# Taking the 2 KB strip off the first load of a DMA-bound rotation

## The chip, the core and the metric

The kernel runs on one core of a Trainium2 chip. The metric is the time of one execution on the device in microseconds (us). Repeated executions lie within some 0.3% of each other. The "span" of a profile runs from the first to the last instruction of the core; the measured times are some 1.8 us longer.

## The reference

```python
x = np.random.randn(32, 3, 256, 256).astype(np.float32)
def reference(x):
    return np.rot90(x, k=2, axes=(-2, -1)).astype(np.float32)
```

A rotation by 180 degrees reverses the 65,536 values of each of the 96 images. 25.17 MB go in and 25.17 MB come out. Nothing is computed.

## The kernel before

The 96 images are handled in three groups of 32. A group lies in the SBUF, the core's own memory, as 128 partitions of 16,384 floats (64 KB): each image takes four partitions. VectorE, one of the core's compute engines, reverses each partition in place, block by block, through a small tile T. The store then writes the four partitions of an image in reverse order.

```python
E = L // 4            # 16384 floats, one partition of a group
J = E // 8            # 2048, a block of the copies
N = E // 32           # 512 floats: the 2 KB strip
...
def load(t, g, lo=0, hi=E):
    nc.sync.dma_start(out=t[:, lo:hi], in_=x4[g][:, lo:hi])
def store(t, g):
    nc.sync.dma_start(out=o4[g][:, ::-1, :], in_=t[:, :])
def inside(t):
    for lo in range(0, E // 2, J):
        hi = E - lo - J
        copy(T[:, :], back(t, hi, hi + J))
        copy(t[:, hi:hi + J], back(t, lo, lo + J))
        copy(t[:, lo:lo + J], T[:, :])

load(A, 0, 0, N)      # the strip: 128 rows of 2 KB
load(A, 0, N, E)      # the rest of group 0: 128 rows of 62 KB
load(Bt, 1)
load(Ct, 2)
for g, t in enumerate((A, Bt, Ct)):
    inside(t)
    store(t, g)
```

There is a tile for each group, so no load waits for a tile to come free. Loads and stores are all issued by the sync engine, on one queue.

## Time and profile before

| | before |
|---|---|
| time, median of the first 3 runs | 123.02 us (122.84 to 123.25) |
| span of the profile | 121.1 us |
| VectorE busy | 44.2 us, 36% |
| the DMA queue's packets, share of 16 engines' span | 97.4% |
| DMA transfers | 7: two for load A, one each for loads B and C, three stores |

The profile is read here in three ways. The page gives shares and the landing time of each transfer, counted from its issue. The windows give what the DMA engines moved in a stretch. The packet records of the trace give each row's start and duration: the large rows, sorted by start and taken sixteen at a time, one for each DMA engine, show the kernel as 48 rounds. The page's lines stand in the prediction below.

### The profile page before, as it was taken

Reading aid. Unit: us, or ns where it says so; the run is one execution under the profiler, and the core shown is the slowest. Engines: PE = TensorE matmul, PEld = TensorE weight load, DVE = VectorE, ACT = ScalarE, POOL = GpSimd, SP = SyncE. Lnnn points to the kernel's source line nnn. Section 1 sums busy time; section 2 is a strip of 40 time slices with the busy share of each in tenths; the row PEclk is TensorE's granted clock in tenths of the full one; section 3 lists DMA queues with packets and bytes.
Section 4 is the critical chain, followed back from the end, with each engine's and each line's share of the span. In section 5 each row is a group of like instructions: output and inputs, shape, how many; then the busy total and the mean of one; then the engine's idle time right before and its main releaser. Section 6 shows DMA issues by size and latency. Waiting matters only on the chain.

```text
span 121.1 us, 94 instructions
## 1 busy us (share of the span) xinstructions
DVE 44.2 (36%) x36; POOL 0.2 (0%) x4
## 2 busy tenths in 40 slices
DVE  0000000599994199998039999600000000000000
POOL 0000000000000000000000000000000000000000
DMA  9977987897799879978989977997799779977980
GB/s 359 399 336 336 650 356 336 346 693 346 346 411 628 346 346 476 563 346 346 346 346 476 563 346 346 563 476 346 346 584 455 346 346 606 433 346 346 671 368 0
DMA packets 1008, 50.33 MB, mean 416 GB/s; under 512 B 112, under 2 KB 112, under 8 KB 240
## 3 DMA queue, kind: packets, MB, share of 16 engines
q1 hardware_dynamic: 1008, 50.33, 97.4%
HBM read 25.17 MB, written 25.17 MB: 416 GB/s over the span
## 4 chain that ended last, share of the span: by engine, by line
DMA 33%; DVE 25%; another core or an unknown queue 4%; issue 1%; SPq 1%; DVEq 0%
DMA Bt<-in_x_dram 33%; DVE T L53 8%; DVE Ct L53 8%; DVE Bt L53 8%; SPq L56 1%; DVEq L53 0%
## 5 line engine op out<-in xcount | busy, mean ns | idle before, releaser
L53 DVE COPY T<-A 128x2048 f32<-128x2048 f32 x4 | 4.9, 1227 | 22.7 <-DMA A<-in_x_dram 22.6
L53 DVE COPY T<-Ct 128x2048 f32<-128x2048 f32 x4 | 4.9, 1227 | 5.4 <-DMA Ct<-in_x_dram 5.3
L53 DVE COPY T<-Bt 128x2048 f32<-128x2048 f32 x4 | 4.9, 1227 | 4.4 <-DMA Bt<-in_x_dram 4.3
L53 DVE COPY Bt<-T 128x2048 f32<-128x2048 f32 x4 | 4.9, 1227 | 0.1
L53 DVE COPY A<-T 128x2048 f32<-128x2048 f32 x4 | 4.9, 1227 | 0.1
L53 DVE COPY Ct<-Ct 128x2048 f32<-128x2048 f32 x4 | 4.9, 1227 | 0.1
L53 DVE COPY Bt<-Bt 128x2048 f32<-128x2048 f32 x4 | 4.9, 1227 | 0.1
L53 DVE COPY A<-A 128x2048 f32<-128x2048 f32 x4 | 4.9, 1227 | 0.1
L53 DVE COPY Ct<-T 128x2048 f32<-128x2048 f32 x4 | 4.9, 1227 | 0.1
L89 POOL MEMSET const-bfloat16-1.0<- 128x1 bf16 x1 | 0.1, 101 | 0.0
L89 POOL MEMSET const-uint8-127<- 128x1 uint8 x1 | 0.1, 101 | 0.0
L89 POOL MEMSET const-float32-0.0<- 128x1 f32 x1 | 0.1, 98 | 0.2 <-issue 0.2
L89 POOL MEMSET const-float32-1.0<- 128x1 f32 x1 | 0.1, 98 | 0.0
## 6 DMA issues: line engine op xcount, KB each, us to landing
A<-in_x_dram SPq DMA_DIRECT2D x1, 7936.0 KB, 21.4
A<-in_x_dram SPq DMA_DIRECT2D x1, 256.0 KB, 2.8
Bt<-in_x_dram SPq DMA_DIRECT2D x1, 40.3
Ct<-in_x_dram SPq DMA_DIRECT2D x1, 60.3
out_dram<-A SPq DMA_DIRECT2D x1, 43.9
out_dram<-Bt SPq DMA_DIRECT2D x1, 43.8
out_dram<-Ct SPq DMA_DIRECT2D x1, 42.7
```

The costliest lines, as they stand in the source:

```text
L53: tc.keep_in_program_order(nc.vector.tensor_copy(out=dst, in_=src))
L56: nc.sync.dma_start(out=t[:, lo:hi], in_=x4[g][:, lo:hi])
L89: nc = _bacc.Bacc("TRN2", target_bir_lowering=False, num_devices=1)
```

## The change

The intent is one transfer and one issue fewer: load A becomes one transfer of 8 MB like the others.

```diff
-    N = E // 32
...
-    def load(t, g, lo=0, hi=E):
-        nc.sync.dma_start(out=t[:, lo:hi], in_=x4[g][:, lo:hi])
+    def load(t, g):
+        nc.sync.dma_start(out=t[:, :], in_=x4[g])
...
-    load(A, 0, 0, N)
-    load(A, 0, N, E)
+    load(A, 0)
     load(Bt, 1)
     load(Ct, 2)
```

## The prediction

> **What bounds the kernel now.** I read the first parts of the page for the shares, then the issues with their landing times, then the windows, to see whether the DMA engines ever run below their full rate.
>
> ```profile
> span 121.1 us, 94 instructions
> DVE 44.2 (36%) x36; POOL 0.2 (0%) x4
> ...
> DMA packets 1008, 50.33 MB, mean 416 GB/s; under 512 B 112, under 2 KB 112, under 8 KB 240
> ...
> q1 hardware_dynamic: 1008, 50.33, 97.4%
> ...
> A<-in_x_dram SPq DMA_DIRECT2D x1, 7936.0 KB, 21.4
> A<-in_x_dram SPq DMA_DIRECT2D x1, 256.0 KB, 2.8
> Bt<-in_x_dram SPq DMA_DIRECT2D x1, 40.3
> Ct<-in_x_dram SPq DMA_DIRECT2D x1, 60.3
> out_dram<-A SPq DMA_DIRECT2D x1, 43.9
> ```
>
> VectorE (DVE) works for 36% of the span, the one DMA queue for 97.4%. Of the 1,008 packets, 112 are under 512 B (16 for each of 7 transfers: the completion marks), 128 are the strip's 2 KB rows, and 768 are whole rows of 62 or 64 KB. The landing times run from each issue. Load C is issued at 2.11 us in the timeline and lands at 62.4. The store of A is issued at 37.76 us and lands at 81.7, although its data were ready at 37.7: it stood behind load C. So the queue is served in order, and a store gets its turn long after it was issued.
>
> The windows show the same. Columns: stretch, its length, VectorE busy (instructions), GpSimd busy, clock, DMA share, GB/s.
>
> ```profile
> 1.70:2.60 0.90, 0.00 (x0) 0.00 (x0) 1.00 0.72 162
> ...
> 6.00:22.00 16.00, 0.00 (x0) 0.00 (x0) 1.00 1.00 430
> ...
> 41.00:58.00 17.00, 14.72 (x12) 0.00 (x0) 1.00 1.00 432
> 58.00:62.00 4.00, 0.00 (x0) 0.00 (x0) 1.00 1.46 508
> ...
> 81.00:119.00 38.00, 0.00 (x0) 0.00 (x0) 1.00 1.00 433
> ```
>
> Loads alone (6 to 22, 41 to 58) and stores alone (81 to 119) run at 430 to 433 GB/s with a DMA share of 1.00. There is no idle stretch to fill. (A window counts a packet's bytes where it ends, so the 508 is an edge effect.) The page's chain of waits puts 33% on load B and 25% on VectorE copies, but this is the chain of issues; the store that it leads to was issued at 77.59 us while the queue still had some 42 us of work. I do not take it as the bound. **The bound is the bytes through the queue, from the first packet to the last.**
>
> In the trace's packet records, each of the 16 DMA engines moves 8 strip rows, then 48 large rows one after the other, the next within a few ns of the end of the one before. A 64 KB row takes 2.418 us, a 62 KB row 2.342 us, a strip row 0.084 us. Sum for one engine: 8 x 0.084 + 8 x 2.342 + 40 x 2.418 = 116.1 us. First packet at 1.75 us, last end at 119.97: 118.2 us in all. The 2.1 us beyond the sum are start-up (0.6 us), one slow last row of load C on every engine (mean 3.55 instead of 2.418 us, so 1.1 us, where loads turn to stores), and the engines' spread of some 0.5 us, of which the mean engine sees half.
>
> **What the Trainium skill says.** (1) "DMA: Bandwidth & Descriptors", section "Where 436 GB/s comes from": 16 ports of 256 bits at 850 MHz give 435.2 GB/s. The trace agrees: 16 x 65,536 B in 2.418 us is 433.7 GB/s. Full rows are already at that ceiling, so the change cannot make a row faster. (2) The same page, "Queues, rings and completion order": on each engine descriptors are consumed in ring order. The landing times above agree. (3) The same page, "Anatomy of one DMA", gives a fixed cost of about 2 us for each DMA, measured there on the other issuing path and mostly completion latency. Were that paid in series, one DMA fewer would save about 2 us. This trace disagrees: the small transfer is followed on each engine by the next row within some 10 ns of its completion mark. (4) "SBUF — State Buffer", "SBUF: two separate sides": DMA and compute engines do not contend. The trace agrees: 432 GB/s with VectorE busy 14.72 of 17 us, 433 with it idle.
>
> **The change, part by part.**
> - *One issue fewer on the sync engine.* The two issues of A take 0.86 us together in the timeline, so about 0.43 us leaves the sync engine before load B is issued. Load B's rows are not wanted before about 21 us. Worth 0.
> - *The strip's 128 rows and 16 marks go.* Per engine 8 x 0.084 + 0.009 = 0.68 us, on the path.
> - *The 8 rows of load A grow from 62 to 64 KB.* Per engine 8 x (2.418 - 2.342) = 0.61 us, on the path. The bytes are the same; net of these two, -0.07 us.
> - *The start-up is met by 64 KB rows instead of 2 KB rows.* Before: the first strip row starts at a mean of 1.92 us over the engines, the first large row at 2.954. That is 1.03 us for rows that take 0.67 at the steady pace, so 0.36 us lost (18 of the 128 rows took over 0.1 us, some 0.6). The first round of 62 KB rows took 2.562 on average, another 0.22 lost. Together 0.58 us. After: the same start at 1.92, since the first issue does not move, and then one loss L on the first round of 64 KB rows. I cannot read L from this trace. Nothing lost would be L = 0; if the two losses were simply merged, 0.58; the worst stall this trace has is 1.1 us. I choose 0.45: large rows should hide part of the first latency that the short rows showed in full.
> - *The sum.* Before, the first row of load B starts at a mean of 21.967 us. After: 1.92 + 8 x 2.418 + 0.45 = 21.71, so 0.25 us earlier; with L from 0 to 1.1 between 0.7 earlier and 0.4 later. Everything after it (40 rows per engine at 2.418, the turn from load to store, the tail of 1.1 us after the last packet) stands as it is and moves along. 123.02 - 0.25 is 122.8 us.
> - *VectorE* starts its first copy when A is in, now at 22.63 us, then at about 22.4; the first store is issued at about 37.5 instead of 37.8. Its turn in the queue comes at about 61.5. Worth 0.
>
> **The rivals.**
> 1. *The strip is a primer that earns its place.* Whoever tuned this kernel put it there. Without it, all 16 engines begin with a 64 KB read at once, perhaps in closer step, and stall more. For it: the first round after the strip ran unevenly (2.342 to 2.949 us), and the spread of the engines' starts (0.47 us in the first large round, 0.36 between first strip packets) is set up by the strip. Against it: load B and load C are whole-row transfers with the same addresses' spacing, and run at the full 2.418 us. A stall also spreads the engines by itself. If true as a one-time cost: 0.5 to 1 us, so 123.3 to 124. If every load row of A slowed by 10%: 8 x 0.24 = 1.9 us, 124.9; to lose 2% (2.46 us) would need more than that, or a slowdown that lasts into B and C.
> 2. *Each transfer has a fixed price in series.* Then about 2 us are saved, 121 us. The gapless packets speak against it. Even with L = 0 and no strip, only 0.7 us is available, under 0.6%; so faster by 2% is all but ruled out.
> 3. *A later start is hidden or absorbed.* If the first 0.2 us gained were met by a queue running dry before the first store, they would be lost again. But the store of A is issued 24 us before its turn, the store of C at 77.6 us while A's store is still moving. So a gain or a loss at the front goes straight through to the end, and the result should be the front's difference, plus noise.
> 4. *The slow round where loads turn to stores changes.* It costs 1.1 us on every engine and I do not know what causes it. If it depended on how the engines stand to each other, it could shrink or grow by some tenths. This widens the range both ways.
>
> **Range and chances.** The three runs of before lie within 122.84 to 123.25, so the noise is about 0.2 us. L from 0 to 1.1 gives -0.7 to +0.4 us, the turn and noise add some 0.3 either way, and rival 1 adds weight above. Predicted 122.8 us, 8 times in 10 between 122.3 and 123.6. Faster by over 2% (below 120.6) 0.01, within 2% 0.94, slower by over 2% (above 125.5) 0.05, which is rival 1 in its lasting form.
>
> **What would show it.** In the profile after: 864 packets (1,008 less 128 strip rows and 16 marks), none between 512 B and 8 KB, the same 50.33 MB; one issue of A that lands some 21.5 us later, and the first copy at 22.2 to 22.6 us. Windows of loads alone and stores alone still at 430 to 433 GB/s. The first rows of load A at 2.418 plus about 0.45 us, all later ones but the last of load C at 2.418. The prediction is wrong if rows of load A take clearly more than 2.418 us beyond the first round, if loads B or C change pace, if the slow round at the turn changes by more than some tenths, or if the end does not move by what the first copy moved.

## The result, and the profile after

| | before | after |
|---|---|---|
| median of 6 runs each | 122.83 us (122.78 to 123.25) | 122.91 us (122.80 to 123.01) |
| span of the profile | 121.1 us | 121.2 us |
| load B's first row, mean start over the 16 engines | 21.967 us | 21.946 us |
| slow last row of load C, mean | 3.550 us | 3.549 us |
| end of each engine's last row, mean | 119.72 us | 119.69 us |

The ratio of the times is 0.9999 (95% interval 0.9984 to 1.0014). It is the same.

The page after, with the lines that answer to those of before in the prediction:

```profile
span 121.2 us, 91 instructions
DVE 44.2 (36%) x36; POOL 0.2 (0%) x4
...
DMA packets 864, 50.33 MB, mean 415 GB/s; under 512 B 96, under 2 KB 96, under 8 KB 96
...
q1 hardware_dynamic: 864, 50.33, 97.4%
...
A<-in_x_dram SPq DMA_DIRECT2D x1, 21.8
Bt<-in_x_dram SPq DMA_DIRECT2D x1, 40.7
Ct<-in_x_dram SPq DMA_DIRECT2D x1, 60.7
out_dram<-A SPq DMA_DIRECT2D x1, 44.1
```

The 128 strip rows and their 16 marks are gone from the packets, and the bytes are unchanged. The landing times of loads B and C seem to be 0.4 us later, but they are counted from issues that now come 0.45 us sooner (load B at 1.18 instead of 1.63 us). On the clock of the span they land where they did. The timeline shows the issues:

```profile
0.73 0.39 SPq L55 DMA_DIRECT2D A<-in_x_dram  x1
1.18 0.42 SPq L55 DMA_DIRECT2D Bt<-in_x_dram  x1
1.64 0.43 SPq L55 DMA_DIRECT2D Ct<-in_x_dram  x1
22.57 1.23 DVE L52 COPY T<-A 128x2048 f32<-128x2048 f32 x1 [22.57 <-DMA A<-in_x_dram]
```

The first copy starts at 22.57 us; before it was 22.63. So nearly nothing was gained at the front. The windows of the kernel after (stretch, its length, VectorE busy, GpSimd busy, clock, DMA share, GB/s):

```profile
1.70:2.60 0.90, 0.00 (x0) 0.00 (x0) 1.00 3.49 1165
...
6.00:22.00 16.00, 0.00 (x0) 0.00 (x0) 1.00 1.00 434
...
41.00:58.00 17.00, 14.72 (x12) 0.00 (x0) 1.00 1.02 439
58.00:62.00 4.00, 0.00 (x0) 0.00 (x0) 1.00 1.34 475
...
81.00:119.00 38.00, 0.00 (x0) 0.00 (x0) 1.00 0.99 428
```

The long stretches still move at the full rate. A row's bytes are counted whole where it starts, not where it ends as the prediction said. That is why the first window has 1165 GB/s (sixteen rows of 64 KB begin in it), and why the others stray by a few per cent from 433: one round more or less at an edge. For anything finer the packet records decide.

They say where the start-up went. Before, the first large rows began at 2.954 us and took 2.563 us on average instead of 2.342; in front of them the strip's rows had taken 0.95 us for each engine instead of 0.67. After, the first large rows began at 1.899 us and took 3.140 us on average instead of 2.418. From the next round on, each row took 2.418 us until the turn to the stores. So the first round lost 0.72 us where the strip (0.28) and the round after it (0.22) had lost 0.50.

### The profile page after: what moved, and what is told of

Read it like the earlier page. It is cut to its first block, busy times and chain, and to the rows that moved or that the text cites. A ratio compares the mean times of both kernels' runs of the same rounds, so it can differ in the third digit from the quotient of the medians.

```text
span 121.2 us, 91 instructions
## 1 busy us (share of the span) xinstructions
DVE 44.2 (36%) x36; POOL 0.2 (0%) x4
## 4 chain that ended last, share of the span: by engine, by line
DMA 34%; DVE 25%; another core or an unknown queue 4%; issue 1%; SPq 0%; DVEq 0%
DMA Bt<-in_x_dram 34%; DVE T L52 8%; DVE Bt L52 8%; DVE Ct L52 8%; SPq L55 0%; DVEq L52 0%
## 6 DMA issues: line engine op xcount, KB each, us to landing
out_dram<-A SPq DMA_DIRECT2D x1, 44.1
```

## The experiments

The theory: the strip's own price in the steady stream is about 0.07 us, and its place at the head saves about as much of the start-up, so that taking it away moves nothing; what the front gains or loses goes through to the end. The rivals: each transfer has a large fixed price in series, which the start-up hid; the strip is a primer worth more than its cost; slack further back absorbs the gain. The first four kernels ran on one chip with eleven runs of the kernel before (median 122.90 us), the next four with eleven (122.96), the last four with eleven or twelve (122.99). All twelve gave right results.

The columns below come from the packet records: the mean start of load B's first row (where the front ends), the mean duration of the last load row in front of each turn from loads to stores, and the mean end of the engines' last rows.

| run | load B begins, us | last large load row before a turn, us | last rows end, us | time, us | ratio to before (95%) |
|---|---|---|---|---|---|
| before | 21.967 | 3.55 | 119.72 | 122.83 | |
| after | 21.946 | 3.55 | 119.69 | 122.91 | 0.9999 |
| tail | 21.950 | 3.76 | 119.89 | 123.14 | 1.0012 (1.0000 to 1.0024) |
| narrow | 22.351 | 3.56 | 120.12 | 123.56 | 1.0046 (1.0031 to 1.0061) |
| wide | 21.910 | 3.65 | 119.97 | 123.04 | 1.0010 (0.9998 to 1.0022) |
| sixteen | 23.123 | 2.42 | 119.80 | 123.44 | 1.0048 (1.0033 to 1.0062) |
| delay | 26.378 | 3.59 | 124.18 | 127.47 | 1.0362 (1.0343 to 1.0381) |
| cturn | 21.911 | 3.30 (62 KB) | 119.67 | 123.05 | 1.0012 (0.9992 to 1.0033) |
| actst | 21.936 | loads and stores mixed | | 132.45 | 1.0763 (1.0733 to 1.0794) |
| moredve | 21.921 | 3.60 | 119.72 | 123.43 | 1.0029 (1.0009 to 1.0049) |
| latec | 21.996 | 3.42 | 119.62 | 122.94 | 0.9999 (0.9982 to 1.0015) |
| latebc | 21.924 | 3.63 | 119.75 | 123.03 | 1.0005 (0.9990 to 1.0021) |
| order | 21.976 | 2.97 and 2.49 | 119.20 | 122.69 | 0.9982 (0.9963 to 1.0002) |
| order_strip | 21.950 | 3.19 and 2.46 | 119.37 | 122.74 | 0.9977 (0.9960 to 0.9993) |

Seven kernels load A in one undelayed transfer (after, cturn, moredve, actst, latec, latebc, order). Their load B begins at 21.911 to 21.996 us, 21.944 on average. The two profiles with the 2 KB strip at the head have 21.967 and 21.950. The difference of 0.01 us is smaller than the spread among equal fronts.

**The strip at the other end of load A (tail).**

```diff
-    load(A, 0, 0, N)
-    load(A, 0, N, E)
+    load(A, 0, 0, E - N)
+    load(A, 0, E - N, E)
```

> The strip at the tail of load A instead of at its head: the first rows are large ones as in the changed kernel, and the strip's own price is met in the steady stream. Theory (the strip costs what its rows take, 0.68 us per engine, less 0.61 us that the large rows shrink by, and its place at the head bought back some 0.1 us of start-up): the first round loses about 0.72 us as in the changed kernel, load B's first row starts at a mean of about 22.0 us, time within 0.2 us of both kernels. Rival (each transfer has a fixed price of about 2 us in series, which the strip at the head hid in the start-up): about 125 us, with a gap or slow rows at about 21 us. Rival primer (the strip at the head saves as much as it costs): 0.1 us slower than the changed kernel, not to be told from the theory by the time, only by the packet records.

The issues of this run (size, us from issue to landing):

```profile
A<-in_x_dram SPq DMA_DIRECT2D x1, 7936.0 KB, 21.2
A<-in_x_dram SPq DMA_DIRECT2D x1, 256.0 KB, 21.4
```

The strip was issued right behind the large part and landed behind it. All of its 128 rows took less than 0.1 us, 0.084 in the median. Load B began at 21.950 us. A fixed price of 2 us in series is ruled out. The time was 0.12% (0.15 us) over before. In this profile the slow row at the turn was 0.2 us longer than in before, which would account for it; whether the strip had a part in that is not known.

**Other strip widths at the head (narrow, wide).**

```diff
-    N = E // 32
+    N = E // 128      # narrow: 512 B rows
+    N = E // 4        # wide: 16 KB rows
```

> Strip rows of 512 B instead of 2 KB, at the head. Theory: the rows take about 0.03 us each, 8 per engine 0.22 us, and the large rows shrink by 0.15; the start-up loss is between 0.5 and 0.75 us as with either kernel; time within 0.3 us of before. Rival primer by amount of data (the strip hides start-up in proportion to its bytes): the start-up loss is near the 0.72 us of no strip. Rival primer by number of rows: near 0.58 us.

> Strip rows of 16 KB instead of 2 KB, at the head. Theory: the steady price of a split is the same 0.07 us; the start-up loss between 0.58 and 0.72 us; time within 0.3 us of before. Rival primer by amount of data: start-up loss below 0.58 us, time up to 0.4 us less than before.

The narrow strip missed its expectation of 0.3 us: 0.46% is 0.57 us. First its windows, then those of the kernel before:

```profile
1.70:2.20 0.50, 0.00 (x0) 0.00 (x0) 1.00 0.44 130
2.20:2.60 0.40, 0.00 (x0) 0.00 (x0) 1.00 5.36 1789
2.60:3.60 1.00, 0.00 (x0) 0.00 (x0) 1.00 0.86 325
```

```profile
1.70:2.20 0.50, 0.00 (x0) 0.00 (x0) 1.00 0.67 78
2.20:2.60 0.40, 0.00 (x0) 0.00 (x0) 1.00 0.79 266
2.60:3.60 1.00, 0.00 (x0) 0.00 (x0) 1.00 2.87 1133
```

With 512 B rows the engines are busy for 0.44 of the first window, then wait: the last sixteen strip rows ended between 2.10 and 2.25 us, and the first large rows began at 2.23 at the earliest and 2.565 on average. The issue of the large part starts at 1.16 us, 0.43 after that of the strip; the first rows of each issue follow it by 1.0 to 1.1 us (1.753 after 0.73, 2.232 after 1.16). A strip that is done sooner than the next issue takes effect leaves the engines dry, here for some 0.4 us. The last sixteen rows of the 2 KB strip ended between 2.92 and 3.18 us, so it is long enough not to. The narrow strip did not soften the start-up either: its first round of large rows took 3.007 instead of 2.399 us. These 0.4 us are still there where load B begins (22.351 instead of 21.967) and in the mean end of the last rows; the rest of the 0.57 is not accounted for. The wide strip had the same front as no strip to within 0.04 us, so more bytes in the strip save nothing. Neither is a better primer.

**Load A in sixteen transfers (sixteen).**

```diff
-    load(A, 0, 0, N)
-    load(A, 0, N, E)
+    for k in range(16):
+        load(A, 0, k * (E // 16), (k + 1) * (E // 16))
```

> Load A as 16 transfers of 4 KB rows. Theory (a split costs only its additional packets, some 8.4 ns each, worked out from 84 ns for 2 KB against 2.342 us for 62 KB, and 9 ns for each completion mark): 120 more rows and 15 more marks per engine, 1.0 + 0.14 us, so about 1.1 us slower than before, 123.9 us. The 16 issues of some 0.43 us run ahead of rows that take 1.28 us per transfer. Rival (a fixed price of 2 us for each transfer in series): about 30 us slower, 153 us.

The front lost what was expected: load B began at 23.123 us, 1.18 later than in the kernel after, for 15 more transfers and 120 more rows per engine. So a split is cheap, some 0.08 us for a transfer with 8 rows per engine. But the time was only 0.48% over before. The slow last row of load C, 3.55 us in the two kernels compared, took 2.42 here. This gave back 1.1 us and was not foreseen. In the profiled execution (123.24 us, the fastest of its four and 0.35 over the profiled one of before) the last rows ended at a mean of 119.80 us, 0.08 later than in before; 0.30 of the 0.35 is the stretch from the last packet to the end of the span, 1.43 instead of 1.13 us.

**A front that is late by a known amount (delay).**

```diff
+    tc.keep_in_program_order(nc.vector.memset(A[:, :E // 4], 0.0))
     load(A, 0)          # the kernel after; its loads kept in program order
```

> The changed kernel with a 128x4096 memset on VectorE that load A waits for, so that the whole stream starts later by the memset's time (some 2 to 4 us, worked out from 1.23 us for a 128x2048 copy). Theory (the stream is gapless from its first row to its last, so what the front gains or loses reaches the end undiminished): start-up loss again about 0.72 us, the end moves by as much as the first row moved, within 0.2 us. Rival (slack further back absorbs what the front loses): the end moves by clearly less.

Its timeline:

```profile
1.65 3.47 DVE L67 MEMSET A<- 128x4096 f32 x1 [1.65 <-PEq L88]
5.15 0.38 SPq L55 DMA_DIRECT2D A<-in_x_dram  x1
```

The first row moved from 1.740 to 6.160 us, by 4.42. Load B moved by 4.43, the mean end of the last rows by 4.48. The ratio of 1.0362 on 122.96 us is 4.45 us. The stream has no slack: what the front loses is lost at the end. That a gain would pass in the same way is argued from the same gapless rows and not tested, but no gain had to be absorbed: load B began only 0.02 us sooner.

**More work on VectorE (moredve).**

```diff
             copy(T[:, :], back(t, hi, hi + J))
+            copy(T[:, :], back(t, hi, hi + J))
```

> The changed kernel with each first copy done twice: 4.9 us more VectorE work per tile, so stores are issued at about 42.6, 62 and 82.5 us. Theory (VectorE has over 20 us of slack): within 0.2 us of before. As to the slow last row of load C: if it goes with the issue of store B, which then falls 4.9 us later, after the turn, the slow row moves or goes, worth up to 1.1 us; if it goes with the turn itself, it stays at about 3.55 us.

4.9 us more for each tile, 14.7 us in all, moved the time by 0.29%, some 0.4 us, with an interval of 0.1 to 0.6. That is more than the 0.2 us expected, but the excess does not lie where VectorE works: the spans of the four executions are 121.0 to 121.3 us, as those of before in the same rounds (121.0 to 121.6), and the mean end of the last rows was 119.72 us, as in before. The time outside the span was 2.2 us instead of 1.8 in all four; why is not known. Inside the span VectorE has its slack. The slow row stayed at 3.60 us, so it does not go with the issue of store B.

**The turn from loads to stores (cturn, latec, latebc, order, order_strip).** The run with sixteen transfers had shown that the slow row is not a fixed price. It is equal before and after, so it is no part of the change's result; but it is 1.1 us, more than anything the strip could be worth.

```diff
# cturn: the kernel after, the strip cut from the tail of load C
-    load(Ct, 2)
+    load(Ct, 2, 0, E - N)
+    load(Ct, 2, E - N, E)
# latec: load C issued only when A is in
# (here and in latebc the loads are kept in program order)
+    copy(Ct[:, :1], A[:, :1])
     load(Ct, 2)
# latebc: loads B and C issued late
+    tc.keep_in_program_order(nc.vector.memset(Bt[:, :], 0.0))
     load(Bt, 1)
+    tc.keep_in_program_order(nc.vector.memset(Ct[:, :E // 16], 0.0))
     load(Ct, 2)
# order: load C queued behind store A (order_strip: the same, with the strip)
-    load(Ct, 2)
         store(t, g)
+        if g == 0:
+            load(Ct, 2)
```

> The changed kernel with the 2 KB strip cut from the tail of load C, so that strip rows and not a large row are the last before the stores. Theory A (the slow last row of 3.55 us is a fixed wait for the first store rows): the strip rows carry about 1.1 us of wait, time within 0.2 us of the changed kernel plus 0.07. Theory B (the large row is slowed in proportion while stores begin behind it): the wait falls to some 0.04 us and the time to about 121.9 us. The case that neither explains: the last large row of load C is slow although rows of its own load's kind follow it.

> The changed kernel with load C issued only once A has landed (it waits for a one-column copy from A to C on VectorE), at about 23 us instead of 1.6. Its turn in the queue is at 41 us, so no row moves later. Theory as to the slow last row of load C (it goes with how the loads were queued: with load A in sixteen pieces, whose loads B and C were issued at 15 and 16 us, it was gone): the slow row falls from 3.55 to about 2.42 us, time about 121.9 us. Rival (what matters there is the small rows of load A, or nothing that the issue times touch): the row stays at about 3.5 us, time within 0.2 us of before.

> The changed kernel with loads B and C issued at about 15 and 16 us, as they were with load A in sixteen pieces (they wait for a 128x16384 and a small memset on VectorE), load A one transfer. Theory (issue times): the slow last row of load C falls to about 2.42 us, time about 121.9 us. Rival (the small rows of A): 3.5 us, time within 0.2 us of before.

In cturn the last large row was slow (3.30 instead of 2.34 us) although eight small rows per engine stood between it and the stores: theory A and theory B both fall. Late issues do not remove it either. Load C was issued at 22.91 us in latec:

```profile
22.91 0.33 SPq L55 DMA_DIRECT2D Ct<-in_x_dram  x1
```

and its last row still took 3.42 us. In latebc, with issues at 17.95 and 19.03 us, it took 3.63. The theory that went by issue times fell in both.

> The changed kernel with load C queued behind the store of A, so that the queue turns from loads to stores twice (before store A and before store B) and once from a store to a load. Theory (a turn from loads to stores costs 1.1 us, the other turn some 0.5 to 0.7 like a start): about 1.7 us slower than the changed kernel, 124.6 us. Rival (the slow row comes once for a reason other than the turn): within 0.3 us of before.

> The kernel before, with its strip, and load C queued behind the store of A as in the run before this one: a second profile of the strip's front, and a second look at that order. Theory (the strip moves the front by next to nothing, and a turn from loads to stores costs less the fewer load rows came before it in one go: 24 rows 1.1 us, 16 rows 0.55, 8 rows 0.07): first large rows of load B at a mean of 21.9 to 22.0 us, slow rows of about 0.55 us before store A and below 0.1 before store B, time within 0.2 us of the same order without the strip, about 122.7 us. Rival (the strip does help, and its first profile had one accidental slow round): load B's rows 0.1 to 0.3 us earlier than without the strip. Rival as to the turns (chance): the two slow rows have other sizes, 1.1 us among them.

The issues of order, with load C and the stores in their new turns:

```profile
out_dram<-A SPq DMA_DIRECT2D x1, 24.3
Ct<-in_x_dram SPq DMA_DIRECT2D x1, 43.3
out_dram<-Bt SPq DMA_DIRECT2D x1, 43.1
```

Store A lands 24.3 us after its issue instead of 44.1, as it no longer stands behind load C. Two turns to stores were expected to cost more than one. They cost less: 0.55 and 0.07 us beyond 2.418 in order, 0.77 and 0.05 in order_strip, against 1.13. The turn back from stores to a load cost nothing (rows of 2.42 us on both sides of it). Both orders are faster by about 0.2%. For order_strip the interval (0.9960 to 0.9993) lies below 1; for order it touches 1. By the turns the gain should be 1.13 less 0.63, 0.5 us, in order and 1.13 less 0.82, 0.3 us, in order_strip; the ratios give 0.2 and 0.3. The mean end of the last rows moved by 0.5 and 0.35 us, but the engines' last rows end 1.1 and 1.3 us apart instead of 0.54, and the latest ends no sooner than in before (120.10 and 120.32 us against 119.97). The profiled execution was the slowest of each kernel (123.04 and 123.24 us), so neither span shows the gain. That the turns make the gain of the faster executions is therefore likely, but not shown. These are the best versions found, and the strip makes no difference between them: ratios of 0.9982 without and 0.9977 with it.

That a turn costs more the more load rows came before it in one go (8, 16 and 24 rows: below 0.1, 0.55 to 0.77, 1.0 to 1.3 us) fits these runs. It does not fit the run with sixteen transfers, where 16 large rows behind 128 small ones were followed by a turn without a slow row. The cause stays open.

**Stores on a second queue (actst).**

```diff
-        nc.sync.dma_start(out=o4[g][:, ::-1, :], in_=t[:, :])
+        nc.scalar.dma_start(out=o4[g][:, ::-1, :], in_=t[:, :])
```

> The changed kernel with the three stores issued from the scalar engine, so that they stand in a second queue and begin at about 38 us between rows of load C. Theory (the bytes set the time): load C lands later, at about 80 us, the copies of C end at about 96, and the last store still has bytes to move then, so within 0.5 us of before, less up to 1.1 us if the one slow round at the turn does not occur. Rival (mixed reading and writing is slower than either alone): some per cent slower.

The theory fell and its rival held: 7.6% slower. Windows of this run:

```profile
3.60:22.00 18.40, 0.00 (x0) 0.00 (x0) 1.00 1.00 435
...
60.00:80.00 20.00, 0.00 (x0) 0.00 (x0) 1.00 0.96 347
...
100.00:129.00 29.00, 6.08 (x5) 0.00 (x0) 1.00 0.87 375
```

While loads and stores mix, the rate falls from 435 to 347 GB/s with the engines busy; the rows of load C took 2.8 to 3.3 us on average. Load C was therefore late (its last row ended at 88.2 us, its last completion mark at 90.7, behind one more row of a store), the last store was issued only at 106.25, and in the last window the queues ran short of work (0.87). One queue that keeps loads and stores apart is the better arrangement here.

## Why the prediction was right

The bound was right. The stream of rows set the time, and delay shows that a late front is late at the end by as much.

*One issue fewer on the sync engine: worth 0.* Right. Load B was issued 0.45 us sooner and began at the same time, within 0.02 us.

*The strip goes (0.68 us), the rows grow (0.61 us): net -0.07.* The tail run is the test of this term by itself, and agrees as far as it can be seen: it began load B at 21.950 us with the strip, against 21.944 without. 0.07 us is at the edge of what these profiles resolve.

*The start-up loss L, chosen as 0.45 us.* This is the term that was mis-sized. By the prediction's own sum, 1.92 + 8 x 2.418 + L is 21.946, so L was 0.68 us (0.65 to 0.73 over the seven kernels with this front). The reason for the choice, "large rows should hide part of the first latency that the short rows showed in full", was wrong: the first large round lost 0.72 us, the strip and the round after it 0.50. The prediction had read these as 0.58, because it took 1.92 us, the mean start of the sixteen earliest strip rows, for the mean first start of the sixteen engines. The strip's rows took 0.95 us for each engine before 2.954, which puts that start at about 2.0 (an estimate from these two numbers). What makes the first large rows slow is not shown. With L at 0.68 instead of 0.45, the gain of 0.25 us at load B becomes 0.02. The range for L, 0 to 1.1 us, held it. The prediction's other wrong reading, that a window counts bytes where a packet ends, entered no sum.

*Everything behind moves along.* Right: rows of 2.418 us, a slow row of 3.55 and 3.55 us, and last rows that end at 119.72 and 119.69 on average.

*VectorE: worth 0.* Right in the two kernels. The first copy started at 22.57 us rather than at the 22.4 expected, because of L.

*The rivals.* The primer (1) exists in a small size. The strip at the head lost 0.28 us itself, 0.22 in the first large round, and some 0.06 in the fifth, which was slow in both profiles with this strip (2.398 and 2.412 instead of 2.342 us). With its price of 0.07 this makes 0.63 us, against the 0.72 of the plain front in the kernel after. The strip's front also began about 0.1 us later (2.0 instead of 1.90), which is no more than the mean start scatters among the seven equal fronts (1.90 to 2.04 us). So the strip about pays for itself. No row after the first round of load A was slow in the kernel after, so the lasting form of this rival is out. The fixed price in series (2) is out by tail and sixteen. Absorbed later (3): out by delay, which tested it for a loss. The turn (4) did not change with the strip.

The predicted 122.8 us was 0.1 below the measured 122.91, less than the runs scatter. That it came so near is partly luck: it was counted from 123.02 us, the median of three runs, and from the 122.83 of all six it would have been 122.6. The direction of that small gain is not confirmed: the ratio's interval reaches from -0.16% to +0.14%.

## What to carry to other kernels

When one queue of large transfers never runs dry, one transfer more or less cost here only its additional rows and marks, below 0.1 us of 123; look at the landing times and at the gaps between rows before expecting more from merging transfers. A small transfer at the head should last until the next issue takes effect: the 512 B strip did not, left the engines dry for some 0.4 us, and was 0.5% slower. A front that differs in its parts can still end at the same time, so compare where the next transfer begins, and compare it with the scatter of several equal fronts before giving a meaning to 0.05 us.

## What the Trainium skill lacked or had wrong

- "DMA: Bandwidth & Descriptors", section "Anatomy of one DMA — SWDGE (gpsimd) path": the fixed cost of about 2 us for each DMA (measured there on the other issuing path) says nothing of what a transfer costs that stands in a queue behind another. Here that was some 0.08 us (15 more transfers with 120 more rows per engine: 1.18 us).
- "DMA: Bandwidth & Descriptors", section "Issuing engines are not separate DMA queues": it says that issuing from several engines only saves issue time. It lacks what it can cost to let loads and stores interleave: 347 instead of 435 GB/s in the mixed stretch, and 7.6% of the time in the run with stores on a second queue.
- No page read for this has the price of a turn from loads to stores on one queue: the last large load row took 3.3 to 3.8 us instead of 2.34 or 2.42 after 24 large rows, 2.97 to 3.19 after 16, 2.46 to 2.49 after 8, and 2.42 in the one case where 128 rows of 4 KB came first.
